# A hybrid attention and gated-linear-attention layer on one core: warm-up at the start, earlier tables, another layout of memory for the output passes, and projections ahead of the last products

## The chip, the cores and the metric

The kernel runs on one core of a Trainium2 chip. The metric is the device time of one execution in microseconds, and smaller is better. The core has a matrix engine (TensorE, PE in the profile), a vector engine (VectorE, DVE), an engine for activations (ScalarE, ACT), a general one (GpSimd, POOL) and a queue engine that issues the DMAs (SyncE, SP).

## The reference

2048 tokens of 1024 numbers go through one layer. `norm_mix`, `ple_norm` and `final_norm` are weights of root-mean-square norms.

```python
u = rmsnorm(h, norm_mix);  z = u @ w_in           # one projection for both groups
aq, ak, av, gq, gk, gv, g_low, za, zg = split(z)
aq, ak = partial_rope(aq, positions), partial_rope(ak, positions)   # sine and cosine tables
y_att = swa_sink_attention(aq, ak, av, sinks)     # window of 128 tokens
log_g = log_sigmoid(g_low @ w_gate_up + b_gate) / 16
y_gla = rmsnorm(gla_chunked(gq, gk, gv, log_g), gla_norm)
h = h + concat(y_att * silu(za), y_gla * silu(zg)) @ w_out
gate = sigmoid(rmsnorm(h, ple_norm) @ w_ple_gate)
out = rmsnorm(h + gate * (p @ w_ple_proj), final_norm)
```

Everything is float32. Each product is made of three products of a high and a low part of the operands.

## The kernel before, in words

The work has two phases. The first makes everything up to the gated outputs of both groups; the second is the output projection, the gate and the last norm.

**First phase.** The 16 tiles of 128 tokens are done in two halves of eight. For a tile, `u_norm` and `u_scale` (L328 to L342) norm the 128x1024 tile `xt`, and `u_tr` (L343) transposes it on TensorE and splits it into `uth` and `utl`. `load_w` (about L262 to L293) loads weights in pieces called `raw`, and splits each into a high part `wh` (ScalarE, L286) and a low part `wl` (VectorE or GpSimd, L288); the parts are also stored to `wd` in DRAM, for the second half. The first weights are `wA`, 272 columns wide: 256 for keys and values of the attention and 16 for `g_low`. `section_a` multiplies a tile by `wA`, turns the keys by the rotary tables `csC` and `csS`, splits them into `kst`, and transposes `kst` (L392). `constants()`, called inside the first `section_a`, loads small constants and `w_gate_up` (into `wu`, split to `wup`, L193 to L201) and makes the rotary tables (L204 to L244).

**Second phase.** Three passes: 0 and 1 add the two halves of the output projection to the residual, 2 makes the gate. A pass multiplies blocks of two row tiles (a pair; the first and, in passes 0 and 1, the last block have two pairs, n = 0 and 1) by a 1024x1024 weight with seven products in place of eight, in the order `ORDER = 0, 4, 1, 6, 5, 2, 3`. A product is 12 matmuls of 128x512 (L774 to L776). Its right operand `T` was made in the first phase and stored in DRAM; a T is loaded in four pieces of 512 KB (L122). Its left operand `c` comes from sums of pieces `y` (passes 0, 1) or `hT` (pass 2) on VectorE, split by ScalarE and VectorE. `xt` (L814) is the residual in passes 0 and 1, `u` (L829) holds product 0 for later. Pass 2 is `gate_block`: `load_p` loads a piece `pi` of the input `p` and transposes it (L901), `load_r` loads the residual `hr`, `proj` multiplies `pi` by `w_ple_proj` (L911 to L913, loaded and split by `load_wq`), `gated` makes sigmoid, product, sum and sum of squares, and `finish` scales by the last norm and stores. The last block does product 3 in two halves of 256 columns (`halves`).

**What sets the order.** The order on each engine is that of a scheduler which simulates the engines' times when the program is built and takes what it finds ready; the code's order sets what comes first among equals. On the chip each engine then works in this fixed order. SP issues nearly all DMAs, in order, on eight lanes in turn: a DMA waits for the one eight before it. Memory is handed out by pools; a tile in a pool waits until the tile that held its place is no longer used. Pools on the right side of the memory (`kvp`, `rawp`) are closed in the second half's last group, and that room goes to the second phase first.

## Time and profile before

| | us |
|---|---|
| median of 3 runs | 1906.24 (1900.41 to 1909.64) |
| profiled execution | 1904.04 |
| its span, first to last instruction | 1902.3 |
| TensorE busy | 1814.7 (95%) |
| VectorE, ScalarE, GpSimd busy | 1203.3, 961.1, 699.3 |
| mean granted clock of TensorE | 0.990 |

TensorE is busy nearly all the time, so what counts is where it is not and what released it then. In a row of the timeline the start comes first and then the duration of one instruction, or of a run of equal ones; `x8` is their number, and a bracket tells the idle time before it and which engine, tile and line ended it. Matmuls overlap, so a duration is longer than the distance to the next one. In a window's row the busy time of each engine stands with its number of instructions, and then the granted clock of TensorE (1.00 is full), the busy share of the DMA engines and GB/s. Rows of SP with `SPq` tell when a DMA was issued, not when it landed.

### The profile page before, as it was taken

The numbers are of one execution on the slowest core, as the hardware profiler recorded it, in microseconds if no ns is written. First come the engines' busy times: TensorE is split into PE (matmuls) and PEld (weight loads), VectorE is DVE, ScalarE is ACT, GpSimd is POOL, SyncE is SP. The second block draws the span as 40 slices with busy tenths as digits, with TensorE's granted clock in tenths as the row PEclk, the third lists the DMA queues.
The fourth block names the chain that finished last, engine by engine and source line by source line (L and its number), as shares of the span: only waits on it lengthen the run. The fifth ranks groups of instructions, "written<-read, shape, count | busy, mean of one in ns | idle before, by whom it ended". The sixth has DMA issues, their size and how long they took to land. (4 is left out here: it accounts for less than half of the span.)

```text
span 1902.3 us, 32715 instructions
## 1 busy us (share of the span) xinstructions
PE 1814.7 (95%) x11297; PEld 1612.9 (85%) x11297; DVE 1203.3 (63%) x2663; ACT 961.1 (51%) x2598; POOL 699.3 (37%) x916
## 2 busy tenths in 40 slices
PE   6999999999999999999999999999899999998997
PEld 6989898998898889898888988988788888787886
DVE  6454785466556474578766756574667667665864
ACT  5544666465557464456654655563422244453543
POOL 5442554534526362544455445352200010102432
PEclk9999999999999999999999999999999999999998
DMA  8332442415324352655576566565685966884542
GB/s 281 122 101 81 147 136 92 155 53 170 97 66 143 102 180 90 199 146 174 178 205 206 163 195 182 160 195 192 230 281 194 324 237 219 313 309 151 179 139 83
DMA packets 326741, 326.78 MB, mean 172 GB/s; under 512 B 23137, under 2 KB 259825, under 8 KB 326321
## 3 DMA queue, kind: packets, MB, share of 16 engines
q1 hardware_dynamic: 326576, 324.70, 52.5%
q8 instruction: 89, 1.46, 0.3%
q14 instruction: 76, 0.61, 0.1%
HBM read 186.08 MB, written 138.54 MB: 171 GB/s over the span
## 5 line engine op out<-in xcount | busy, mean ns | idle before, releaser
L85 PE MATMUL acc<-wh,uth 128*128 128x256 f32 (+1 forms) x1664 | 476.8, 287 | 14.5 <-DVE m L563 4.5
L86 PE MATMUL acc<-wl,uth 128*128 128x256 f32 (+1 forms) x1664 | 472.6, 284 | 6.2 <-DMA wl<-wd 6.0
L87 PE MATMUL acc<-wh,utl 128*128 128x256 f32 (+1 forms) x1664 | 471.1, 283 | 0.0
L85 PEld LDWEIGHTS acc<-wh,uth 128*128 128x128 f32 x1664 | 316.0, 190 | 25.6 <-ACT v L522 5.9
L86 PEld LDWEIGHTS acc<-wl,uth 128*128 128x128 f32 x1664 | 315.7, 190 | 12.9 <-DMA wl<-wd 8.6
L87 PEld LDWEIGHTS acc<-wh,utl 128*128 128x128 f32 x1664 | 315.7, 190 | 2.0
L460 POOL TENSOR_TENSOR pq<-pq,pmask 128x512 fp32r<-128x512 f32 x128 | 178.2, 1408 | 292.9 <-ACT pq L67 285.8
L85 PE MATMUL acc<-uth,wh 128*128 128x512 f32 x512 | 204.3, 399 | 4.8 <-DVE m L563 3.8
L87 PE MATMUL acc<-uth,wl 128*128 128x512 f32 x512 | 201.7, 394 | 0.3 <-DMA wl<-wd 0.3
L86 PE MATMUL acc<-utl,wh 128*128 128x512 f32 x512 | 201.9, 394 | 0.0
L774 PE MATMUL acc<-T,c 128*128 128x512 f32 (+1 forms) x344 | 135.5, 395 | 6.7 <-ACT u L829 6.3
L775 PE MATMUL acc<-T,c 128*128 128x512 f32 (+1 forms) x344 | 135.1, 393 | 0.0
L776 PE MATMUL acc<-T,c 128*128 128x512 f32 (+1 forms) x344 | 135.0, 393 | 0.0
L446 ACT ACTIVATE s<-s,sm 128x128 f32<-128x128 f32 x256 | 99.7, 391 | 51.1 <-DVE sm L442 51.1
L85 PEld LDWEIGHTS acc<-uth,wh 128*128 128x128 f32 x512 | 96.4, 188 | 26.8 <-DVE m L563 5.2
L859 POOL TENSOR_TENSOR ssh<-ssh 128x1 f32<-128x1 f32 x16 | 3.3, 205 | 313.8 <-ACT junk L858 313.8
L288 POOL TENSOR_TENSOR wl<-raw,wh 128x512 fp32r<-128x512 f32 (+1 forms) x82 | 109.6, 1367 | 20.0 <-ACT wh L286 10.2
L87 PEld LDWEIGHTS acc<-uth,wl 128*128 128x128 f32 x512 | 96.1, 188 | 22.5 <-DMA wl<-wd 0.7
L86 PEld LDWEIGHTS acc<-utl,wh 128*128 128x128 f32 x512 | 96.2, 188 | 18.7
L67 ACT ACTIVATE c<-s 128x512 fp32r<-128x512 f32 x72 | 45.1, 629 | 111.1 <-DVE s L104 32.4
L774 PE MATMUL o<-T,c 128*128 128x512 f32 (+1 forms) x252 | 99.3, 394 | 0.0
L775 PE MATMUL o<-T,c 128*128 128x512 f32 (+1 forms) x252 | 98.6, 391 | 0.0
(289 smaller groups left out, 4409.7 us busy)
## 6 DMA issues: line engine op xcount, KB each, us to landing
T<-td SPq DMA_DIRECT2D x84, 512.0 KB, 9.4
wd<-wh SPq DMA_DIRECT2D x20, 1024.0 KB, 5.6
wd<-wl SPq DMA_DIRECT2D x20, 1024.0 KB, 6.3
wh<-wd SPq DMA_DIRECT2D x80, 256.0 KB, 5.4
wl<-wd SPq DMA_DIRECT2D x80, 256.0 KB, 5.5
raw<-in_w_in SPq DMA_DIRECT2D x68, 256.0 KB, 5.6
y<-yts SPq DMA_DIRECT2D x64, 256.0 KB, 5.6
td<-th SPq DMA_DIRECT2D x48, 256.0 KB, 2.8
```

The lines of the kernel that those rows point to most:

```text
L67: act.activation(h, src, AF.Copy)
L85: pe.matmul(ps, lhs_h(k), rhs_h(k), start=(k == 0), stop=False)
L86: pe.matmul(ps, lhs_h(k), rhs_l(k), start=False, stop=False)
L87: pe.matmul(ps, lhs_l(k), rhs_h(k), start=False, stop=(k == nk - 1))
L288: eng.tensor_tensor(wl[:, ks_, 0:n], raw[:, :, 0:n], wh[:, ks_, 0:n], op=ALU.subtract)
L446: act.activation(s[:, j, :], s[:, j, :], AF.Exp, bias=ng[:, j:j + 1], accum_out=su[:, j:j + 1])
L460: pool.tensor_tensor(pq[:, 2 + i, :].rearrange("p (h n) -> p h n", h=4), pq[:, i, :].rearrange("p (h n) -> p h n", h=4), pmb, op=ALU.mult)
L774: pe.matmul(ps, c[:, 0, k, :], t[:, 0, k, sl], start=(first and k == 0), stop=False, skip_group_check=more)
L775: pe.matmul(ps, c[:, 0, k, :], t[:, 1, k, sl], start=False, stop=False, skip_group_check=more)
L776: pe.matmul(ps, c[:, 1, k, :], t[:, 0, k, sl], start=False, stop=(k == 3), skip_group_check=more)
L859: pool.tensor_tensor(ss[:, 0:1], ss[:, 0:1], ss[:, 1:2], op=ALU.add)
```

## The change

Six edits, all in how and when things are done; what is computed stays.

1. Ahead of everything, 14 matmuls of a zero tile `cold` (bfloat16, 128x512) run on TensorE.
2. The rotary tables become a function of their own, called right after the first tile's transposes and ahead of the norm of the third.
3. `load_w` loads new weights wider than 256 columns (only `wA`) in pieces of one 128-row block instead of two: 16 DMAs instead of 8. `raw` becomes a tile of 512 columns, with ten of them instead of nine.
4. The pools of the second phase: `tpr`, on the right, has room for two T instead of three, `tpb` for five instead of four; the tiles of `x2` (15 instead of 17) go to a pool on the right, opened with `tpr`; `c` and the tiles of `load_wq` have pools of their own; `pi` has a single buffer; the results `q` of `gate_block` go from `x2` to `x2b`.
5. `load_wq` moves from the last block of pass 1 to the block before it. The first `load_p` of a block moves to its start.
6. In the last block both projections come at product 6, ahead of products 5, 2 and 3; `finish` of the block's first row comes at product 2.

```diff
@@ start
+        cold = cp.tile([P, 512], BF16, name="cold")
+        dve.memset(cold, 0.0)
+        ps = pt("o")
+        for i in range(14):
+            pe.matmul(ps, cold[:, 0:P], cold, start=True, stop=True)
@@ pools' tiles
     def x2(name, shape=(P, 4, P), dtype=F32):
-        return p2p["xpb"].tile(list(shape), dtype, name=name, tag="x2", bufs=17)
+        return p2p["xpa"].tile(list(shape), dtype, name=name, tag="x2", bufs=15)
...
         for i in which:
-            T[i] = p2p["tpr" if i in ORDER[:3] else "tpb"].tile(
-                [P, 2, 4, 512], F32R, name=f"T{i}", tag="T", bufs=3 if i in ORDER[:3] else 4)
+            T[i] = p2p["tpr" if i in ORDER[:2] else "tpb"].tile(
+                [P, 2, 4, 512], F32R, name=f"T{i}", tag="T", bufs=2 if i in ORDER[:2] else 5)
...
-        rawp = kvs.enter_context(tc.tile_pool(name="rawp", bufs=9, side="right"))
+        rawp = kvs.enter_context(tc.tile_pool(name="rawp", bufs=10, side="right"))
@@ constants()
+        def rotary_tables():
 
             pos_f = wk.tile([16, P], F32, name="pos_f", tag="w1", bufs=8)
@@ load_w
-            for k0 in range(0, KD, 2):
-                ks_ = slice(k0, k0 + 2)
+            kn = 2 if n <= 256 or saved is not None else 1
+            for k0 in range(0, KD, kn):
+                ks_ = slice(k0, k0 + kn)
...
-                raw = rawp.tile([P, 2, SW], F32, name="raw", tag="raw")
+                raw = rawp.tile([P, 512], F32, name="raw", tag="raw")[:, 0:kn * n].rearrange("p (k n) -> p k n", k=kn)
...
-                eng = dve if fast and k0 % 4 == 0 else pool
+                eng = dve if fast and k0 % (2 * kn) == 0 else pool
@@ first phase
         u_tr(0, 0)
+        rotary_tables()
         u_norm(0, 2)
...
                     kvs.close()
-                    p2p["tpr"] = p2r.enter_context(tc.tile_pool(name="tpr", bufs=1, side="right", reuse_waits="tile"))
+                    for name in ("tpr", "xpa"):
+                        p2p[name] = p2r.enter_context(
+                            tc.tile_pool(name=name, bufs=1, side="right", reuse_waits="tile"))
                     T = [None] * 7
-                    load_T(0, ORDER[:3], T)
+                    load_T(0, ORDER[:2], T)
@@ second phase
-        for name in ("xpb", "tpb", "fs"):
+        for name in ("tpb", "cpl", "xpb", "wqp", "fs"):
             p2p[name] = p2.enter_context(tc.tile_pool(name=name, bufs=1, reuse_waits="tile"))
-        load_T(0, ORDER[3:], T)
+        load_T(0, ORDER[2:], T)
...
-            pi = x2("pi", (P, DPLE))
+            pi = fs.tile([P, DPLE], F32, name="pi", tag="pi", bufs=1)
...
-            qs = [[x2(f"q{i}", (P, 512)) for i in range(4)] for _ in prs]
+            qs = [[x2b(f"q{i}") for i in range(4)] for _ in prs]
...
                 elif i == 2:
-                    pps = proj(pTs[n, 0], banks())
+                    pps = state.get(0) or proj(pTs[n, 0], banks())
                     gated(n, 0, 0, pps, s2)
                     gated(n, 0, 1, pps, s2)
+                    finish(n, 0, s2)
                     if last:
-                        state["s"] = s2
-                        state["p"] = proj(pTs[n, 1], [pt("t"), pt("t")])
-                        state["s1"] = sums()
-                        gated(n, 1, 1, state["p"], state["s1"])
-                    else:
-                        finish(n, 0, s2)
+                        state["s"] = sums()
+                        gated(n, 1, 1, state[1], state["s"])
...
-                    if not posts and two:
-                        load_wq()
-                if i == (5 if two else 6):
-                    for h in range(1 if two else 2):
-                        pTs[n, h] = load_p(2 * prs[n] + h)
-                        hrs[n, h] = load_r(2 * prs[n] + h)
+                if i == 5 and two:
+                    hrs[n, 0] = load_r(2 * prs[n])
...
+            if two:
+                for n in range(2):
+                    pTs[n, 0] = load_p(2 * prs[n])
+            else:
+                for h in range(2):
+                    pTs[0, h] = load_p(2 * prs[0] + h)
+                    hrs[0, h] = load_r(2 * prs[0] + h)
             state = {}
...
-                gated(n, 1, 0, state["p"], state["s1"], slice(0, 256))
-                gated(n, 1, 0, state["p"], state["s1"], slice(256, 512), 2)
-                finish(n, 0, state["s"])
-                finish(n, 1, state["s1"])
+                gated(n, 1, 0, state[1], state["s"], slice(0, 256))
+                gated(n, 1, 0, state[1], state["s"], slice(256, 512), 2)
+                finish(n, 1, state["s"])
...
                 if i == 6:
                     state["b6"] = ps
+                    state[0] = proj(pTs[n, 0])
+                    state[1] = proj(pTs[n, 1], [pt("t"), pt("t")])
@@ loop over blocks
+            if ps_ == 1 and prs == (3,):
+                load_wq()
```

The scheduler turns these edits into another order. On SP at the start, before (`raw` are weights, `wd` the stores of split weights, `wu` the four loads of `w_gate_up`):

```order
L292 DMA wd_211<-wl 128x2176
L284 DMA raw<-in_w_in 128x2x128 x5
L292 DMA wd_280<-wh 128x8x256
L284 DMA raw<-in_w_in 128x2x128
L193 DMA wu_368<-in_w_gate_up 16x512 x4
L284 DMA raw<-in_w_in 128x2x128 x2
L292 DMA wd_280<-wl 128x8x256
L284 DMA raw<-in_w_in 128x2x256 x5
```

and now:

```order
L333 DMA xt<-in_x 128x1024
L293 DMA raw<-in_w_in 128x2x128 x8
L293 DMA raw<-in_w_in 128x2x256 x5
L301 DMA wd_355<-wh 128x8x256
L199 DMA wu_443<-in_w_gate_up 16x512 x2
L301 DMA wd_355<-wl 128x8x256
L199 DMA wu_443<-in_w_gate_up 16x512 x2
```

The loads of `wu` went behind seven more loads of weights (two of 128 KB and the five of 256 KB in the last row of before) and, two of them, behind the second store.

On SP around the start of the second phase, before (`xt` is the residual, `y` the left operand, `T` the right one; four pieces are one T):

```order
L814 DMA xt_17658<-in_x 128x512
L587 DMA yts_72<-oyg 128x256
L814 DMA xt_17660<-in_x 128x512
L814 DMA xt_17662<-in_x 128x512
L805 DMA y<-yts_61 128x512 x2
L805 DMA y<-yts_62 128x512 x2
L814 DMA xt_17698<-in_x 128x512
L814 DMA xt_17700<-in_x 128x512
L122 DMA T_17560<-td_145 128x2x512 x4
L122 DMA T_17565<-td_145 128x2x512 x4
L122 DMA T_17570<-td_145 128x2x512 x4
L122 DMA T_17575<-td_145 128x2x512 x4
```

and now:

```order
L128 DMA T_17606<-td_162 128x2x512 x3
L128 DMA T_17611<-td_162 128x2x512 x4
L128 DMA T_17616<-td_162 128x2x512 x4
L128 DMA T_17621<-td_162 128x2x512
L596 DMA yts_70<-oyg 128x256
L596 DMA yts_71<-oyg 128x256
L128 DMA T_17621<-td_162 128x2x512 x3
L817 DMA y<-yts_63 128x512 x2
L817 DMA y<-yts_64 128x512 x2
L596 DMA yts_72<-oyg 128x256
L826 DMA xt_17694<-in_x 128x512
L826 DMA xt_17696<-in_x 128x512
```

The first `xt` stood ahead of sixteen pieces of T and now stands behind twenty of them and behind four pieces of `y` of the third block; the twelve `y` of the first two blocks (yts_57 to yts_62) now stand ahead of all of these rows, behind the first two T.

On TensorE at the end of the program, before (`pp` and `t` are banks of the projections, `o` is one half of the last product 3):

```order
L911 MATMUL pp<-wph,pT 128x512
L912 MATMUL pp<-wpl,pT 128x512
L775 MATMUL o<-T_20048,c_21826 128x256
L776 MATMUL o<-T_20048,c_21826 128x256
L913 MATMUL pp<-wph,pT 128x512
L911 MATMUL pp<-wph,pT 128x512
L912 MATMUL pp<-wpl,pT 128x512
L913 MATMUL pp<-wph,pT 128x512
L911 MATMUL pp<-wph,pT 128x512
L912 MATMUL pp<-wpl,pT 128x512
L913 MATMUL pp<-wph,pT 128x512
```

and now, at the place where the projections end and product 5 begins:

```order
L924 MATMUL t<-wpl_19478,pT 128x512
L925 MATMUL t<-wph_19477,pT 128x512
L923 MATMUL t<-wph_19489,pT 128x512
L924 MATMUL t<-wpl_19490,pT 128x512
L925 MATMUL t<-wph_19489,pT 128x512
L786 MATMUL o<-T_20112,c_21865 128x512
L787 MATMUL o<-T_20112,c_21865 128x512
L788 MATMUL o<-T_20112,c_21865 128x512
```

The projections ended the program; now product 5 (T_20112), product 2 and both halves of product 3 come behind them, and the last matmul is one of product 3.

## Rows read from the trace of the kernel before

**Rows 1.** The page: busy time, share and instructions by engine; then TensorE in forty slices.
```profile
PE 1814.7 (95%) x11297; PEld 1612.9 (85%) x11297; DVE 1203.3 (63%) x2663; ACT 961.1 (51%) x2598; POOL 699.3 (37%) x916
...
PE   6999999999999999999999999999899999998997
```

**Rows 2.** Waits of TensorE, whole span: line, releaser, us in total, times, longest.
```profile
PE acc L774 <- ACT u L829: 6.3, 2, 4.5
...
PE t L392 <- DVE kst L373: 5.3, 1, 5.3
PE t L901 <- DMA pi<-in_p: 4.1, 1, 4.1
```

**Rows 3.** Timeline of TensorE, 10 to 20 us: start, duration, instruction.
```profile
15.21 0.43 PE L85 MATMUL acc<-wh,uth 128*128 128x272 f32 x1
...
19.08 0.29 PE L85 MATMUL acc<-wh,uth 128*128 128x272 f32 x1
```

**Rows 4.** DMA view, 0 to 40 us: issues, size each, median us to landing.
```profile
raw<-in_w_in SPq DMA_DIRECT2D x13, 256.0 KB, 5.4
...
raw<-in_w_in SPq DMA_DIRECT2D x4, 16.0 KB, 4.5
```

**Rows 5.** Timeline of ScalarE, 6 to 46 us, idle time before in brackets.
```profile
13.12 0.66 ACT L286 ACTIVATE wh<-raw 128x544 fp32r<-128x544 f32 x1 [0.93 <-DMA raw<-in_w_in]
...
40.83 1.28 ACT L238 ACT_TABLE_LOAD   x1
```

**Rows 6.** Timeline of VectorE, 34 to 46 us.
```profile
35.16 0.68 DVE L201 TENSOR_TENSOR wup<-wu,wu 16x512 fp32r<-16x512 f32 x1 [2.01 <-ACT wu L200]
...
44.37 0.29 DVE L373 TENSOR_TENSOR kst<-ks,kst 128x128 fp32r<-128x128 f32 x1
```

**Rows 7.** Window 50 to 55 us: busy by engine, granted clock, DMA share, GB/s.
```profile
50.00:55.00 5.00, 5.00 (x34) 5.00 (x34) 2.14 (x3) 1.75 (x3) 0.74 (x2) 0.73 0.14 54
```

**Rows 8.** Timeline of the DMA queue SP, 0 to 40 us.
```profile
26.50 3.34 SPq L193 DMA_DIRECT2D wu<-in_w_gate_up  x4
```

**Rows 9.** Timeline of TensorE, 1360 to 1380 us.
```profile
1367.68 0.80 PE L774 MATMUL acc<-T,c 128*128 128x512 f32 x1 [4.50 <-ACT u L829]
...
1378.77 0.39 PE L774 MATMUL acc<-T,c 128*128 128x512 f32 x1
```

**Rows 10.** Windows of 5 us behind that stretch.
```profile
1370.00:1375.00 5.00, 5.00 (x16) 4.01 (x15) 1.38 (x2) 0.63 (x1) 0.00 (x0) 0.63 1.05 391
...
1380.00:1385.00 5.00, 5.00 (x24) 4.14 (x23) 0.97 (x2) 0.54 (x1) 0.00 (x0) 1.00 1.05 387
```

**Rows 11.** Timeline of the DMA queue SP, 1300 to 1420 us.
```profile
1351.27 2.02 SPq L814 DMA_DIRECT2D xt<-in_x  x3
...
1363.01 17.91 SPq L122 DMA_DIRECT2D T<-td  x16
```

**Rows 12.** DMA view, 1345 to 1382 us.
```profile
T<-td SPq DMA_DIRECT2D x16, 512.0 KB, 10.8
...
xt<-in_x SPq DMA_DIRECT2D x10, 256.0 KB, 6.0
```

**Rows 13.** Timeline of the DMA queue SP, 1700 to 1735 us.
```profile
1722.43 0.88 SPq L1032 DMA_DIRECT2D raw<-in_w_ple_proj  x2
1723.37 0.42 SPq L897 DMA_DIRECT2D pi<-in_p  x1
```

**Rows 14.** Window 1730 to 1735 us.
```profile
1730.00:1735.00 5.00, 5.00 (x21) 4.01 (x20) 1.26 (x3) 1.19 (x3) 0.20 (x1) 0.79 0.53 186
```

**Rows 15.** Tile `pi`, 1715 to 1735 us: its loads from issue to landing.
```profile
DMA to landing us min/median/max: 4.2/4.5/5.0
```

**Rows 16.** Timeline of TensorE, end of the span.
```profile
1890.13 0.39 PE L913 MATMUL t<-wph,pT 128*128 128x512 f32 x1
```

**Rows 17.** Timeline of ScalarE, end of the span.
```profile
1893.65 1.33 ACT L940 ACTIVATE q<-q,rms 128x512 f32<-128x512 f32 x2
```

More of the change, by code (lines that the diff above doesn't have):

```diff
@@ L285, in load_w @@
                     o += m
-                act.activation(wh[:, ks_, 0:n], raw[:, :, 0:n], AF.Copy)
-                eng = dve if fast and k0 % 4 == 0 else pool
-                eng.tensor_tensor(wl[:, ks_, 0:n], raw[:, :, 0:n], wh[:, ks_, 0:n], op=ALU.subtract)
+                act.activation(wh[:, ks_, 0:n], raw, AF.Copy)
+                eng = dve if fast and k0 % (2 * kn) == 0 else pool
+                eng.tensor_tensor(wl[:, ks_, 0:n], raw, wh[:, ks_, 0:n], op=ALU.subtract)
             if saved is None:
@@ L600, in piece @@
             def piece(name, dtype=F32):
-                return rawp.tile([P, 2 * SW], dtype, name=name, tag="raw")[:, 0:512].rearrange("p (b n) -> p b n", b=4)
+                return rawp.tile([P, 4, P], dtype, name=name, tag="raw")
             def load(ps_, k, c):
@@ L765, in combos @@
                     src = {0: a11, 4: s_, 1: a12, 6: a21, 5: s_, 2: s_, 3: a22}[i]
-                    C[i] = p2p["xpb"].tile([P, 2, 4, P], F32R, name=f"c{i}", tag="c", bufs=8)
+                    C[i] = p2p["cpl"].tile([P, 2, 4, P], F32R, name=f"c{i}", tag="c", bufs=8)
                     split(C[i][:, 0], C[i][:, 1], src)
@@ L1021, in hybrid_block_kernel, with wqt @@
         wq_, fn = [], []
+        def wqt(name, dtype=F32):
+            return p2p["wqp"].tile([P, 512], dtype, name=name, tag=name)
         def load_wq():
             for n, ns in enumerate(NS):
-                fn.append(x2b(f"fn{n}"))
+                fn.append(wqt(f"fn{n}"))
                 nc.sync.dma_start(fn[n], final_norm[ns].partition_broadcast(P))
@@ L1029, in load_wq @@
                 for ns in NS:
-                    hl = [x2b(f"wp{c}", dtype=F32R) for c in "hl"]
+                    hl = [wqt(f"wp{c}{k}{len(wq_[k])}", F32R) for c in "hl"]
                     raw = x2("raw3", (P, 512))
```

## The prediction

> **What bounds the kernel now.** The page first: TensorE is busy for 1814.7 of 1902.3 us, and its row of forty slices is below 9 only at the start, in slice 31 and at the end [rows 1]. A change that leaves the matmuls alone can win at most the 87.6 us in which TensorE is idle, and what the clock loses behind a long idle stretch. The waits of TensorE say which idle time this change can touch [rows 2]: 5.3 us for `kst`, 4.5 of the 6.3 us for `u`, and 4.1 us for `pi`. The middle, where the order of instructions is the same before and now, I cost at no change. Timeline and windows then price each place.
>
> **Start, warm-up.** The first 128x272 matmuls take 0.43 us, later ones 0.29 us [rows 3]: TensorE at the lower and at the higher of its two clock levels. Where this is seen again with 512 columns (below), the matmuls follow each other 0.427 against 0.2265 us apart, 0.2 us more each; for 272 columns that is 0.107. I count 23 of them and 16 transposes that run slowly: 2.5 us, and with the transposes at most 4.2. The fourteen zero matmuls run while nothing else can; at 0.427 us each they are done after some 6 us, ahead of the first tile. But the clock is not all. The first weights come in sixteen DMAs instead of eight, and a DMA of SP waits for the one eight before it. 16 KB loads of `raw` land in 4.5 us where the 256 KB ones need 5.4 [rows 4], so halving a load hardly shortens its turn: eight more turns of 4.5 us on eight lanes are 4.5 us if all of it shows, and nothing if the shorter transfers and the overlap make it good. The last piece of these weights is split at 13.12 us now [rows 5]; I expect 15 to 16. TensorE would then wait where it now runs slowly. I take a gain of 2 us, bounds a loss of 2 and a gain of 4.2.
> "DMA: Bandwidth & Descriptors" in the Trainium skill (Rules for kernel authors) says that many small transfers should be made one large one, since below 64 KB one pays mostly overhead; the 4.5 us of the 16 KB load agree with it. By that rule alone the split costs the whole 4.5 us, and the start loses 0.3 us instead of gaining 2; by the bytes alone it would gain 4.2.
>
> **Start, rotary tables.** TensorE waits 5.3 us for `kst`, which VectorE writes at 44.37 [rows 2, 6]. Just ahead VectorE stood 2.0 us for `wu` [rows 6], and the tables go through a table load of 1.28 us on ScalarE at 40.83 [rows 5]. Behind the wait the clock is at the lower level for a while, a mean of 0.73 still in 50 to 55 us [rows 7]. Some 36 matmuls there cost 0.1 us more each, 3.6 us, and TensorE idles 0.8 us again. That is 9.7 us for the whole place. Now the tables are made between the first tiles' transposes, some 20 us earlier on VectorE, so that stall goes. What is late next is `wu`: its four loads were issued at 26.50, in 3.34 us [rows 8]; now seven more loads of weights, 1.5 MB, stand ahead of them on SP, for two of them a store of 1 MB too, and ScalarE takes `wu` ahead of `kst`. Eight DMAs more at the 0.84 us that an issue takes in that row, and the eight of the split, make some 7 to 10 us, so about 35 us, while TensorE, with 24 us of work from 11 us on, asks for `kst` at 35 to 38. A stall of 0 to 3 us may stay. I take 6 us gained, bounds 1 and 9.7. Both parts of the start together: 8 us.
>
> **From the first to the second phase.** TensorE idles 4.5 us until 1367.68 [rows 2, 9]: `u` (ScalarE) stands behind copies that wait for VectorE. Behind it the window 1370 to 1375 holds 16 matmuls at a granted clock of 0.63, 1380 to 1385 holds 24 at 1.00 [rows 10]; 13 slow ones at 0.2 us more are 2.6 us. So 7.1 us can go. After the change `y` of the first two blocks (twelve loads of 256 KB) goes out some 45 us earlier, so VectorE has less to do here, and I expect this stall to go. But what was ahead is now behind. Of the seven T only two instead of three are loaded ahead, and SP issues twenty pieces of T of 512 KB (10.5 MB) before the first residual `xt`; before, ten `xt` loads were issued from 1351.27 on, ahead of the sixteen pieces at 1363.01 [rows 11]. The DMA engines carry 387 GB/s here at a share of 1.05, so they are full [rows 10]. From about 1347, when room is free for T, 10.5 MB of T, 1.05 MB of `y` and 0.25 MB of `xt` need 11.8 / 0.387 = 30.5 us: the first `xt` is there at about 1378. TensorE has 84 matmuls, 19 us, that need no `xt`, from 1350.5 to 1369.5; product 5 then waits for a bank that VectorE frees only with `xt`. So a new idle stretch of 10 us, until about 1380, and 2.6 us of lower clock behind it. Before, product 5 began at 1378.77 [rows 9]: a loss of 4 us. Bounds: a gain of 7 if `xt` comes in time, as it would if each load took the 6.0 us that `xt` took here before [rows 12], and a loss of 8 if T starts later. Once this is over all T are there, and nothing is late behind it.
> In the Trainium skill, "DMA: Bandwidth & Descriptors" (Queues, rings and completion order) says that on each DMA engine the descriptors of one queue are taken in ring order. By that an `xt` gets no share ahead of T, and the 4 us are lost; without it the 7 would be gained. The 10.8 us of T beside 6.0 us of `xt` [rows 12] do not decide, since no `xt` stood behind so much T.
>
> **Second to third pass.** TensorE idles 4.1 us for `pi` [rows 2], which SP issues at 1723.37, behind the loads of `w_ple_proj` [rows 13]. Behind the wait the clock is 0.79 in 1730 to 1735 [rows 14]; 8 matmuls at 0.2 us more are 1.6 us. Now `w_ple_proj` comes a pass earlier, and so does the first `pi`. With some of the smaller waits there I take 6 us gained, bounds 3 and 9. What hides the rest: `pi` has one buffer now, and SP waits in order until it is free. From one transpose of `pi` to the next TensorE has 26 matmuls or more, 5.9 us; a load of `pi` landed in 4.2 to 5.0 us [rows 15]. So I cost the single buffer at nothing, with 0.9 us of room at the tightest place.
>
> **Tail.** TensorE's last matmul starts at 1890.13, and the span ends 11.8 us after it is over; in between ScalarE scales two pieces of `q` in 1.33 us from 1893.65 on, for the first row of the last block [rows 16, 17]. Now the 24 projection matmuls (5.4 us) stand ahead of product 5, and that row is finished ahead of the last halves. There are as many matmuls; behind the last one there remain an addition, sigmoid, product, sum, sum of squares, scale and store: 9.3 to 9.8 us by the pieces of before. 2 us gained, bounds 0 and 3.
>
> **Sum.** -8 + 4 - 6 - 2 = -12 us. The profiled execution took 1904.04 us (its span 1902.3 and 1.7 around it), 2.2 less than the median of 1906.24. So 1892 from the one and 1894 from the other: **1893 us**.
>
> **Rivals.** (a) The sum as above: 45%. (b) Nothing that can be told: the split loads eat the warm-up and `wu` holds `kst` (-3 for the start instead of -8), and the transition loses 8: -3 + 8 - 6 - 2 = -3, so 1902. For it: DMA is full at both places. Against it: `pi` and the tail hang on neither. 27%. (c) More: `xt` comes in time, -8 - 7 - 6 - 2 = -23, so 1882. For it: `xt` landed in 6.0 us before under the same load; against it the order of SP. 18%. (d) Slower: the single buffer of `pi`. If a load of it lands more than 5.9 us after the transposes before it, SP stands, with `hT` of the next block and `hr` behind it, and TensorE idles in each of six blocks as it now does once, 4.1 us and 1.6 of lower clock: 34 us, 1927. If half the blocks are hit, 1910. Against it: a DMA share of 0.53 there [rows 14], and loads within 5.0 us so far. 10%, of which 7 are slower than the bound.
>
> About 0.5%, 9.5 us, is what a measurement of this kernel can tell from no change: faster is below 1896.7, slower above 1915.8. Of (a) 43 parts of 45 are faster, and (c) with all its 18, and 3 of (b): 64%. Slower 7%, the same 29%. The range goes from (c) to the middle of (b) and (d): 1881 to 1905; that of (a) alone is 1887 to 1899.
>
> **What would show it.** Right: 272-column matmuls of 0.29 us soon after the first, no wait for `kst` over 3 us, granted clock 1.00 in 45 to 55 us; a wait of 8 to 11 us near 1369 that an addition of `xt` on VectorE ends; no wait for `pi`; less than 10.5 us from the last matmul to the end. Wrong: no idle stretch near 1369 (then c); a wait for the first weights, or for `kst` as long as now (then b); a wait for `pi` or `hT` in each block of the third pass (then d).

## The result: slower by half a per cent, not faster

| us | median (runs) | profiled execution, its span |
|---|---|---|
| before | 1907.55 (6) | 1904.04, 1902.3 |
| changed | 1918.50 (6) | 1920.28, 1918.6 |

The ratio is 1.0064 [1.0040, 1.0087], and 1.0055 [1.0037, 1.0072] in a second measurement. 1893 was forecast, in a range up to 1905: the time is outside it, on the side that had a chance of 7%.

To see where it goes I compare the two traces at equal work: for a moment of the kernel before I add up the columns that its matmuls have streamed, and look when the changed kernel has streamed as many (its zero matmuls not counted). The difference is TensorE's lag in us (negative: it is ahead).

| at (us, kernel before) | 24 | 47 | 55 | 100 | 1350 | 1390 | 1722 | 1755 | 1890 |
|---|---|---|---|---|---|---|---|---|---|
| changed | 4.0 | 3.0 | 2.2 | 6.3 | 14.9 | 21.3 | 24.1 | 16.0 | 16.2 |
| before, another execution (e5) | -0.3 | 0.3 | 1.1 | 1.1 | 1.6 | 2.4 | 3.8 | 3.4 | 3.4 |

So the start costs 6.3 us, the long middle 8.6, the transition 6.4, the second pass 2.8; `pi` gives back 8.1; from 1755 to the end nothing changes. These make 16.0 of the 16.3 us by which the spans differ. Of the start's 6.3 us, 2.2 are there at 55 us; the other 4.1 come between 65 and 84 us.

### The profile page after: what moved, and what is told of

It is laid out like the page before. It is cut to its first block, busy times and chain, and to the rows that moved or that the text cites. A ratio compares the mean times of both kernels' runs of the same rounds, so it can differ in the third digit from the quotient of the medians.

```text
span 1918.6 us, 32723 instructions
## 1 busy us (share of the span) xinstructions
PE 1827.5 (95%) x11311; PEld 1619.8 (84%) x11311; DVE 1215.2 (63%) x2666; ACT 963.4 (50%) x2602; POOL 700.5 (37%) x918
## 4 chain that ended last, share of the span: by engine, by line
PE 36%; DMA 7%; DVE 5%; ACT 3%; issue 1%; SPq 1%; POOL 0%; DVEq 0%; ACTq 0%; POOLq 0%
PE acc L91 4%; PE acc L92 4%; PE acc L93 4%; PE acc L786 3%; PE acc L788 3%; PE acc L787 3%; PE o L788 2%; PE o L786 2%; PE o L787 2%; DMA y<-yts 1%; DMA wh<-wd 1%; DMA T<-td 1%; PE sw L788 1%; PE sw L786 1%; PE sw L787 1%
```

## The profile after

The page's first row and TensorE's slices, against [rows 1]:

```profile
PE 1827.5 (95%) x11311; PEld 1619.8 (84%) x11311; DVE 1215.2 (63%) x2666; ACT 963.4 (50%) x2602; POOL 700.5 (37%) x918
...
PE   7999999999999989999989999999889999999997
```

TensorE is busy 12.8 us longer, of which the zero matmuls are 6. Its waits (in total, times, longest), against [rows 2]:

```profile
PE acc L786 <- DVE xt L113: 11.4, 2, 10.8
...
PE t L401 <- DVE kst L382: 3.4, 1, 3.4
...
PE t L355 <- DVE utl L74: 2.3, 2, 1.2
PE t L355 <- DVE xt L348: 1.8, 2, 1.4
```

The wait for `pi` is gone, and so is the long one for `u`. `kst` is still waited for, `xt` of the second phase is now waited for 10.8 us, and the first tiles (`utl`, `xt` L348) have waits of their own.

**Start.** Timeline of TensorE, against [rows 3]:

```profile
5.47 1.75 PE L67 MATMUL o<-cold 128*128 128x512 bf16 x4
7.62 1.32 PE L355 MATMUL t<-identr,xt 128*128 128x128 f32 x8 [0.40 <-DVE xt L348]
10.53 0.59 PE L91 MATMUL acc<-wh,uth 128*128 128x272 f32 x1 [1.59 <-ACT uth L73]
...
12.77 0.28 PE L215 MATMUL t<-identr,pos_f 16*128 16x16 f32 x1 [1.42 <-DVE utl L74]
...
13.38 0.43 PE L91 MATMUL acc<-wh,uth 128*128 128x272 f32 x1
...
17.18 0.29 PE L92 MATMUL acc<-wl,uth 128*128 128x272 f32 x1
...
21.94 0.63 PE L355 MATMUL t<-identr,xt 128*128 128x128 f32 x4 [1.36 <-DVE xt L348]
23.72 0.90 PE L355 MATMUL t<-identr,xt 128*128 128x128 f32 x4 [1.16 <-DVE utl L74]
...
24.65 0.43 PE L91 MATMUL acc<-wh,uth 128*128 128x272 f32 x1
```

The warm-up works: the eight transposes end after 1.32 us. Before, they took 1.97:

```profile
7.46 1.97 PE L346 MATMUL t<-identr,xt 128*128 128x128 f32 x8 [7.46 <-DVE xt L339]
```

Then TensorE has nothing to do, since `uth` and `utl` of the first tile are not there, and the 272-column matmuls begin at the pace of the lower level all the same. Two waits later, from 24.65 on, they are slow once more. The windows (busy by engine PE, PEld, DVE, ACT, POOL; granted clock; DMA share; GB/s) say so too:

```profile
10.00:15.00 5.00, 3.05 (x12) 2.69 (x13) 4.59 (x10) 3.25 (x8) 3.51 (x5) 0.53 0.69 172
...
20.00:25.00 5.00, 2.49 (x16) 2.07 (x15) 4.97 (x9) 1.63 (x6) 3.93 (x6) 0.90 1.03 397
25.00:30.00 5.00, 5.00 (x34) 5.00 (x33) 3.58 (x15) 4.16 (x12) 3.71 (x11) 0.76 0.90 275
...
50.00:55.00 5.00, 4.75 (x23) 4.35 (x23) 4.25 (x6) 3.32 (x9) 2.98 (x10) 0.53 0.34 105
```

VectorE is busy for 4.97 of the 5 us from 20 to 25 while TensorE has half a window's work: the early tables stand among the first tiles. The last row is behind the wait for `kst`; it answers to [rows 7]. What was late there is on the queue SP, against [rows 8]:

```profile
4.59 7.95 SPq L293 DMA_DIRECT2D raw<-in_w_in  x13
12.59 0.43 SPq L333 DMA_DIRECT2D xt<-in_x  x1
...
34.38 1.48 SPq L199 DMA_DIRECT2D wu<-in_w_gate_up  x2
...
37.16 3.32 SPq L199 DMA_DIRECT2D wu<-in_w_gate_up  x2
```

And on ScalarE:

```profile
43.47 0.28 ACT L372 ACTIVATE ks<-acc 128x128 f32<-128x128 f32 x1 [5.55 <-PE acc L93]
...
43.92 0.61 ACT L204 ACTIVATE wup<-wu 16x512 fp32r<-16x512 f32 x1
```

`xt` at 12.59 is the third tile, behind thirteen pieces of weights; `wu` is issued between 34.4 and 40.5, and ScalarE splits it at 43.92, ahead of `kst`.

**Transition.** The queue SP, against [rows 11]:

```profile
1364.66 12.99 SPq L128 DMA_DIRECT2D T<-td  x12
...
1385.05 3.49 SPq L817 DMA_DIRECT2D y<-yts  x4
...
1389.65 7.39 SPq L826 DMA_DIRECT2D xt<-in_x  x10
```

TensorE, against [rows 9]:

```profile
1386.01 0.39 PE L788 MATMUL sw<-T,c 128*128 128x512 f32 x1
1397.23 0.79 PE L786 MATMUL acc<-T,c 128*128 128x512 f32 x1 [10.83 <-DVE xt L113]
1397.82 0.63 PE L787 MATMUL acc<-T,c 128*128 128x512 f32 x1
```

The first `xt` is issued only behind all of T and four `y`, and product 5 begins at 1397.23, which is 1382.3 without the lag of 14.9 that was there already. Behind it the matmuls follow each other 0.427 us apart: the lower level.

**Pass 2 and the tail.** The window that answers to [rows 14] is at full clock without an idle stretch:

```profile
1730.00:1735.00 5.00, 5.00 (x28) 4.13 (x27) 2.72 (x5) 1.51 (x4) 0.00 (x0) 1.00 0.28 105
```

At the end, one row each of TensorE, ScalarE, GpSimd and VectorE; the last matmul starts 12.2 us before the span's end, as in [rows 16] (1902.3 less 1890.13):

```profile
1906.34 0.28 PE L788 MATMUL o<-T,c 128*128 128x256 f32 x1
...
1910.23 1.32 ACT L952 ACTIVATE q<-q,rms 128x512 f32<-128x512 f32 x2
...
1911.40 2.93 POOL L953 TENSOR_TENSOR q<-q,fn 128x512 f32<-128x512 f32 x2
...
1911.46 3.41 DVE L955 SCALAR_TENSOR_TENSOR q<-q,rms,fn 128x512 f32<-128x512 f32 x2 [0.95 <-POOL rms L79]
```

ScalarE's two scalings of the block's first row come at the very end here as in [rows 17], and now GpSimd's and VectorE's last work falls together.

## The experiments

Each median stands beside that of the kernel before, run on the same chip in between. Lags are TensorE's, as above.

### The start: e1, e2, e3, e12

e1 is the changed kernel without edits 1 to 3 (`rotary_tables()` is back in `constants()`):

```diff
-        for i in range(14):
-            pe.matmul(ps, cold[:, 0:P], cold, start=True, stop=True)
...
-            kn = 2 if n <= 256 or saved is not None else 1
+            kn = 2
...
-        rotary_tables()
```

> The changed kernel with the first three edits undone (no zero matmuls, rotary tables back inside the constants, first weights in eight DMAs); the memory of the second phase, pi and the tail stay changed. Theory A (the start loses because the sixteen DMAs push the third tile's load and the loads of wu back): TensorE's lag behind the kernel before, which is 6.3 us at 100 us in the changed kernel, is within 0.5 us of zero there, and the time falls by 6 us to about 1912. If the extra lag of the middle (6.3 to 12 us between 100 and 1300 us) only follows from the start, it goes too: 1907. Rival B (the start is slow for another reason, for example the pool of raw tiles or the other layout): the lag at 100 us stays at 4 us or more, 1917 to 1919.

Measured: 1912.14 (10) against 1910.13 (26), ratio 1.0003 [0.9986, 1.0020]. The lag at 100 us is 0.4 and not 6.3, the 5.3 us for `kst` are back, and the 10.6 us for `xt` stay. The three edits of the start lose time; the rest is about even.

e2 keeps the zero matmuls and the early tables, and takes back the split alone (`kn = 2`).

> The changed kernel with one edit undone: the first weights in eight DMAs again (raw tiles of 544 columns, nine of them). Theory A: the third tile's load is issued at about 10 us instead of 12.6, the waits of 1.4 and 1.2 us at 21 to 24 us go, the loads of wu are issued at about 27 us instead of 34 to 40, and the wait for kst falls under 1 us; the lag at 100 us falls from 6.3 us to between -4 and 0, the time to 1908 to 1912. Rival C (the early rotary tables take VectorE's time just when it is needed for the tiles): the waits at 21 to 24 us stay, lag at 100 us of 4 us or more, 1916 or more.

Measured: 1913.77 (10), ratio 1.0018 [1.0008, 1.0028]. Timeline of SP in e2:

```profile
4.95 4.76 SPq L293 DMA_DIRECT2D raw<-in_w_in  x5
9.75 0.47 SPq L333 DMA_DIRECT2D xt<-in_x  x1
...
27.43 2.25 SPq L199 DMA_DIRECT2D wu<-in_w_gate_up  x4
```

And of TensorE:

```profile
24.61 1.11 PE L355 MATMUL t<-identr,xt 128*128 128x128 f32 x4 [4.11 <-DVE utl L74]
```

With eight DMAs the third tile is issued at 9.75 and `wu` at 27.43, and no wait for `kst` is left: the split made both late. But now the tables stand in VectorE's way, 4.11 us for `utl`. The lag is 7.1 at 24 us, -2.0 at 55 and 0.9 at 100: early tables and zero matmuls together gain no more than they cost (e1 has 0.4 at 100 us). Taking back the split alone removes 5.4 of the start's 6.3 us. "DMA: Bandwidth & Descriptors" in the Trainium skill (Rules for kernel authors) has it that many small transfers should be one large one; this trace agrees, with 2.8 us more until SP comes to the third tile.

One thing more makes the tables dear here. Two of their rows on VectorE in e2, of one form:

```profile
16.89 0.28 DVE L238 SCALAR_TENSOR_TENSOR ra_t<-ra_t 128x128 f32<-128x128 f32 x1
...
21.46 1.34 DVE L239 SCALAR_TENSOR_TENSOR ra_t<-ra_t 128x128 f32<-128x128 f32 x1
```

And what GpSimd does beside the second:

```profile
19.18 4.74 POOL L297 TENSOR_TENSOR wl<-raw,wh 128x512 fp32r<-128x512 f32 x3
```

The row beside GpSimd's splits takes 1.06 us more, and it stands ahead of the `utl` that TensorE waits for. No run takes GpSimd's work away here; e16 below does so at the end of the program.

e3 keeps all of the changed kernel and loads and splits `wu` ahead of the first weights.

```diff
+        def gate_up():
...
+        gate_up()
```

> The changed kernel with one edit more: the four loads of w_gate_up and their split go ahead of the first weights' loads. Theory A: the wait for kst at 47 us (3.4 us) goes, and with it the lower clock in 47 to 54 us (about 4 us); the waits at 21 to 24 us stay or grow by 1 to 2 us, since four more DMAs stand ahead of the third tile. Lag at 100 us 1 to 3 us instead of 6.3, time 1912 to 1915. Rival (kst is late for its own tile, not for wu): the wait for kst stays at 3 us or more, 1918.

Measured: 1915.43 (10), ratio 1.0025 [1.0013, 1.0038]. No wait for `kst`; in its place one of 5.2 us for `uth` at 14.02, since ScalarE splits `wu` first (its timeline):

```profile
12.72 0.62 ACT L209 ACTIVATE wu<-wu 16x512 fp32r<-16x512 f32 x1
13.37 0.60 ACT L73 ACTIVATE uth<-t 128x512 fp32r<-128x512 f32 x1
```

The lag is 4.6 at 24 us, -2.9 at 55 and -0.2 at 100: with the split and the early tables still there, the start's loss is gone once `wu` stands ahead. The third tile is issued at 14.35 here, later than in the changed kernel; so what the split costs is the place of `wu`. (This trace then loses 12.6 us in the middle, from 100 to 1350.)

e12 leaves out the zero matmuls alone.

> The changed kernel without the fourteen zero matmuls (the sixteen DMAs and the early tables stay). Theory A (they gain next to nothing: the clock they bring up is lost again in the waits at 9 to 13 us): lag at 20 us within 0.7 us of the changed kernel's, time the same, 1916 to 1920. Rival (they gain the 2 us forecast for the start): 2 us slower or more, 1920 to 1922.

Measured: 1916.06 (12) against 1909.86 (35), ratio 1.0032 [1.0018, 1.0046]; the changed kernel's intervals overlap with this. The lag is 0.4 at 19 us and 4.1 at 20, where the changed kernel has -0.5 at both: the warm clock gives 0.9 us until 19. The other 3.7 at 20 are a wait that e12 has begun by then and the changed kernel meets a little later, in two parts (1.36 and 1.16 above):

```profile
23.18 0.66 PE L352 MATMUL t<-identr,xt 128*128 128x128 f32 x4 [3.28 <-DVE utl L71]
```

At 24 us e12 has 5.4 against 4.0, at 47 us 1.4 against 3.0, at 100 us 3.2 against 6.3: the gain is gone, and more. In e12 no wait for `kst` is left, though `wu` is issued as late as in the changed kernel (35.4 to 40.5); without the zero matmuls the engines' orders differ, and no run separates the two.

### The transition: e4, e6

e4 opens the pool of the residual first, so that it gets the room that comes free first:

```diff
-        for name in ("tpb", "cpl", "xpb", "wqp", "fs"):
+        for name in ("xpb", "tpb", "cpl", "wqp", "fs"):
```

> The changed kernel with the order of the second phase's pools changed alone: the pool of the residual pieces xt is opened ahead of that of T, so that it gets the room that is free first. SP then issues seven xt ahead of twenty T pieces. Theory A (xt is late since its room, and so its loads, come behind 10.5 MB of T): the wait of 10.8 us for the addition of xt goes, TensorE waits at most 2 us for T instead, the transition's lag falls by 9 to 12 us, time 1907 to 1910. Rival D (the DMA engines are full here, so whatever is put ahead the last comes as late): TensorE waits 5 us or more for T in place of xt, time 1914 to 1918.

Measured: 1917.20 (5), ratio 1.0039 [1.0024, 1.0053]. Timeline of SP in e4:

```profile
1355.77 3.76 SPq L826 DMA_DIRECT2D xt<-in_x  x5
...
1367.93 16.72 SPq L128 DMA_DIRECT2D T<-td  x15
```

And of TensorE:

```profile
1403.47 0.47 PE L786 MATMUL sw<-T,c 128*128 128x512 f32 x1 [1.95 <-issue]
```

`xt` is issued ahead of T now, and the wait of 10.8 us is gone. Part of it comes back: 2.1 us for a `y`, 1.0 for a `c`, and the 2.0 of this row, for which the profile names no releaser. It is not T, whose last piece landed at 1395.58. Just ahead of it VectorE reads the bank `sw`, and before that it stood for a `y`:

```profile
1402.08 0.69 DVE L113 TENSOR_TENSOR s<-y 128x512 f32<-128x512 f32 x1 [1.49 <-DMA y<-yts]
1402.68 0.68 DVE L113 TENSOR_TENSOR xt<-xt,sw 128x512 f32<-128x512 f32 x1
```

It is one of the four `y` of a block that SP issues from 1393.76 on, and from 1385.05 on in the changed kernel. From 1350 to 1420 the lag grows by 3.1 us and not by 6.4 (and by 3.5 in e6 below, where e1 has 4.9). So the order in which room comes free put `xt` behind T, and up to half of the cost goes with it; some of the rest is that `y` comes later now. The time does not show it: the interval overlaps with the changed kernel's, and 1907 to 1910 did not come.

e6 is e1 and e4 together, the changed kernel without its two losses.

> The start of the kernel before (no zero matmuls, rotary tables in the constants, eight DMAs) together with the residual pool ahead of that of T; early y, early pi, early w_ple_proj and the changed tail stay. Theory A: no lag at 100 us, transition 1 to 5 us better than the run with the old start alone, 5 us better from pi: 1902 to 1906, a ratio to before of 0.996 to 0.998. Rival (each gain comes back as a wait for T): ratio 1.000 or more.

Measured: 1908.71 (12) against 1907.64 (29), ratio 1.0003 [0.9990, 1.0016]: even with the kernel before, the rival's ratio. In its trace the transition still costs 3.5 us and the second pass 4.3, which is nearly the 8.1 that `pi` gives back.

### The tail: e7, e16

e7 is e6 with the old order of the last block.

```diff
-                    state[0] = proj(pTs[n, 0])
-                    state[1] = proj(pTs[n, 1], [pt("t"), pt("t")])
...
+                        state["p"] = proj(pTs[n, 1], [pt("t"), pt("t")])
```

> As the run with old start and residual room, with the last block's projections and the finish of its first row where the kernel before has them. Theory A (the changed tail gains nothing: the chain behind the last matmul is as long as before, since product 5, 2 and 3 now end closely behind each other and VectorE and ScalarE have the work of three products behind the last matmul): the same time within 1 us, 11.8 us from the last matmul to the end in both. Rival (it gains the 2 us forecast): 2 us slower.

Measured: 1907.09 (12), ratio 1.0001 [0.9983, 1.0020]: the new tail gains nothing. The last scalings of VectorE in e7:

```profile
1900.05 1.41 DVE L952 SCALAR_TENSOR_TENSOR q<-q,rms,fn 128x512 f32<-128x512 f32 x2 [0.94 <-POOL rms L76]
```

0.7 us each, where the changed kernel takes 1.7. In e16, e6 again, GpSimd's two multiplications by the last norm's weight are left out, so that one row tile lacks that factor.

```diff
                         act.activation(o, o, AF.Copy, scale=rs2)
-                        pool.tensor_tensor(o, o, fn[j], op=ALU.mult)
```

> The changed kernel with the old start and the residual's room first (e6), and in the last block GpSimd's two multiplications by the last norm's weight left out, so that row lacks that factor. In e6 VectorE's last two scalings take 3.41 us (1.7 each), beside two of GpSimd (2.93 us) at the same time; with the old tail, where GpSimd is done before, 1.41 us. Theory A, the new tail's missing 2 us are the two engines in each other's way: VectorE's pair takes 1.4 to 1.5 us, and from the start of the last matmul to the end of the span it is 10.6 to 11.0 us instead of 12.8. Rival, the pair is slow because of something else that stands there (ScalarE's scalings just ahead, the stores): it stays at 3.4, and the end at 12.4 to 12.8 us.

Measured in one execution: span 1899.5. Its last matmul:

```profile
1889.19 0.28 PE L785 MATMUL o<-T,c 128*128 128x256 f32 x1
```

And VectorE's last scalings:

```profile
1894.32 1.41 DVE L952 SCALAR_TENSOR_TENSOR q<-q,rms,fn 128x512 f32<-128x512 f32 x2 [0.95 <-POOL rms L76]
```

1.41 us again, and 10.3 us from the last matmul to the end, where e6 has 12.8 and e7 10.6. The two engines stood in each other's way; without that the new order would be about even with the old one on this kernel, and 1.9 us better than [rows 16] have it (12.2). The old order too ends 10.0 to 10.6 us behind its last matmul in every trace with `pi` in its own buffer (e7, e9, e10, e11, e13, e14); what shortens it there no run isolates. "SBUF — State Buffer" in the Trainium skill (SBUF: two separate sides) says that VectorE and GpSimd share a pair of ports which one holds for a whole instruction while the other is blocked; e16 agrees with it, with 2.0 us for the pair.

### `pi` and the late `wu`, on the kernel before: e9, e13, e8, e10, e11, e14

e9 is the kernel before with `pi` early and in a buffer of its own.

```diff
-            pi = x2("pi", (P, DPLE))
+            pi = fs.tile([P, DPLE], F32, name="pi", tag="pi", bufs=1)
...
+            if two:
+                for n in range(2):
+                    pTs[n, 0] = load_p(2 * prs[n])
```

> The kernel before with one part of the fifth edit alone: pi has its own buffer and a block's first load of it stands at the block's start (w_ple_proj stays where it was, in the last block of pass 1). Theory A (pi was the whole stall between pass 1 and 2, and one buffer costs nothing): the wait of 4.1 us for pi and the lower clock behind it go, 5 to 7 us less lag from 1722 to 1755 us, time 1900 to 1903, ratio 0.996 to 0.9975. Rival (the early pi only shows the next wait, for w_ple_proj's split or hT): less than 2 us.

Measured: 1913.03 (12) against 1909.86 (35), ratio 1.0009 [0.9996, 1.0023]. The wait for `pi` is gone, and the next one takes its place (waits of TensorE):

```profile
PE t L911 <- ACT wph L67: 4.3, 1, 4.3
```

The lag grows by 7.0 us from 1722 to 1755. e13 adds the early `w_ple_proj`, with the room that it needs (15 tiles of `x2`, `q` in `x2b`).

```diff
+            if ps_ == 1 and prs == (3,):
+                load_wq()
```

> The kernel before with pi early in its own buffer and w_ple_proj loaded and split in pass 1, in a pool of its own (room from two fewer x2 tiles; q in x2b); T, y and xt as before, start and tail as before. Theory A (pi and w_ple_proj were one chain: each alone only shows the other): no wait over 1 us for pi or wph at 1720 to 1735 us, 6 to 9 us less lag from 1700 to 1755 us, no loss at the transition: ratio 0.995 to 0.997. Rival (the early loads and fewer x2 tiles take as much elsewhere, as in the changed kernel between 1590 and 1700 us, 3 us there): ratio 0.998 or more.

Measured: 1901.37 (12) against 1905.29 (25), ratio 0.9968 [0.9952, 0.9983]. Neither wait is left, and from 1722 to 1755 the lag falls by 8.0 us. `pi` alone does not bring it, both loads together do; `w_ple_proj` alone was not run. They have a price ahead of that: from 1420 to 1722 the lag grows by 1.9 to 5.0 us in all thirteen traces with both loads early (2.8 in e13), and by 0.2 to 1.4 in the four without.

e8, e10 and e11 move the four DMAs of `wu` alone: in e8 (on e6) and e10 (on e9) right behind the first weights, in e11 (on e9) behind the loads of the third and fourth tile.

```diff
+        wus = [w2("wu0")]
+        for i in range(4):
+            nc.sync.dma_start(wus[0][32 * i:32 * i + 16, :], w_gate_up)
```

> As the run with old start and residual room, and the four loads of w_gate_up issued right behind the first weights, ahead of the third tile, nothing else moved. Theory A (in the kernel before it was VectorE's wait for wu and the late table load behind it that held kst): the wait for kst of 5.3 us falls to 0 to 2.5 us and the lower clock behind it goes or shortens: 3 to 8 us faster than that run. Against it: the third tile comes 3 us later and may make TensorE wait 1 to 2 us at 20 us. Rival (the tables themselves are late, whatever wu does): wait for kst stays above 4 us, no gain.

> The kernel before with pi early and with the loads of w_gate_up right behind the first weights, ahead of the third tile (as in the run with wu behind the weights). Theory A (the two places are independent): 3 to 6 us less from the start beside the 5 to 7 us of pi: 1895 to 1899, ratio 0.992 to 0.996. Rival (the start's gain is given back in the middle, where that run had fallen back from -3.6 to +2.0 us by 1330 us): no better than pi alone.

> As the run before this one, but the loads of w_gate_up stand behind the third and fourth tiles' loads. Theory A (the wait of 2.3 us at 20 us in the run with wu behind the weights came from the third tile pushed back by 3 us): no wait over 1 us at 18 to 24 us, wu is still in time, and the lag at 100 us is 1 to 3 us lower than with wu ahead of the third tile. Rival (wu comes too late again there): a wait for kst of 2 us or more.

Measured: e8 1904.49 (12) against 1907.64 (29), 0.9982 [0.9969, 0.9994], where e6 had 1.0003; e10 1908.88 and e11 1908.11 (12 each) against 1909.86 (35), 0.9998 [0.9985, 1.0011] and 0.9993 [0.9979, 1.0007], where e9 had 1.0009. In all three the wait for `kst` is gone and the lag at 55 us is near -6; e8 has waits of 3.5 us and e10 of 3.0 us for `utl` instead, where ScalarE and VectorE split `wu` early; e11 has 1.2. With the tables where they were, the 5.3 us of [rows 2] hung on where `wu` stands in the queue. Early tables remove them too: e2 has no such wait either, with `wu` at 27.43, about where the kernel before has it. One of the two is enough.

e14 is e13 with `wu` as in e11.

> As the run before, and the loads of w_gate_up behind the third and fourth tiles' loads. Theory A: -4 us at 100 us beside the gain between the passes, ratio 0.992 to 0.996, faster than the kernel before beyond the interval, best of all so far. Rival (gains at the start are lost in the middle): no better than the run before.

Measured: 1898.35 (8) against 1905.29 (25), ratio 0.9957 [0.9941, 0.9972]. It beats both kernels; against e13 the intervals overlap. The 4.7 us by which it leads at 100 us are gone by 1350 (0.8 behind), and so are the 3.4 and 4.0 of e10 and e11 (0.8 and 2.8 behind). TensorE is 7.4 us ahead at 55 us, and the windows behind both places are at full clock:

```profile
50.00:55.00 5.00, 4.75 (x41) 4.51 (x40) 4.18 (x11) 2.90 (x9) 4.10 (x10) 1.00 0.00 0
...
1730.00:1735.00 5.00, 5.00 (x24) 4.14 (x23) 4.79 (x10) 1.28 (x4) 1.25 (x3) 1.00 0.89 311
```

### Both kernels once more: e5, e15

> The kernel before, unchanged, once more with a profile. The changed kernel's TensorE falls back by another 8.6 us between 100 and 1350 us, where the order of instructions is the same as before. Theory A (this part is no effect of the edits: short stretches at the lower clock and waits of 1 to 2 us that come or stay away from one execution to the next): against the first trace of the kernel before this one lags by 3 us or more somewhere in the middle, with other stretches of lower clock. Rival (the edits slow the middle): the two traces of before agree within 1 us at 1330 us.

> The changed kernel once more, on the same chip as the other runs of this group. Theory A: start +6 and transition +6, passes -5, tail 0, and the middle only varies: ratio 1.003 to 1.005 (6 to 9 us), with another trace's middle between 2 and 9 us. Rival (the middle's 8.6 us belong to the change): ratio 1.006 or more and a middle of 8 us again.

e5 took 1907.44, e15 1917.36 (12 runs) against 1905.29 (25). The second trace of the changed kernel has the same lags, 6.3 at 100 us and 14.8 at 1350; the second trace of before is 3.4 us behind the first, 0.5 of it from 100 to 1350, so theory A of e5 does not get its 3 us in the middle. Over all 123 runs the kernel before has a median of 1908.44: its first profiled execution, at 1904.04, was a quick one by 4.4 us, and the changed kernel's, at 1920.28, was 1.8 above its median; some 6 of the 16.3 us are that.

## Why the prediction was wrong, step by step

| term | forecast | trace |
|---|---|---|
| start | -8 | +6.3 |
| middle | 0 | +8.6 |
| transition | +4 | +6.4 |
| second pass | 0 | +2.8 |
| `pi` | -6 | -8.1 |
| tail | -2 | 0 |

- **Start: the step that failed.** It is 14.3 of the 28 us between the forecast's sum of -12 and the 16.0 of the trace. By 24 us, ahead of the place of `kst`, TensorE is 4.0 us behind where 2 ahead was forecast; over that place, until 55 us, it wins 1.8 us and not 6; and 4.1 more are lost by 84 us. Two costs were not in it.
  - The tables were "some 20 us earlier on VectorE", at no price. VectorE is full there, and e2 shows 4.11 us for it. All six traces with early tables lag by 3.6 to 7.1 us at 24 us, with the split or without it, with the zero matmuls or without; the others by 2.7 at most.
  - The split was priced by when the first weights are there. That came out (their last piece is split at 14.37, with 15 to 16 forecast), though not for the reason given: a halved load did land sooner, the 128 KB ones in 2.5 us and the 8 KB ones in 2.2, where the whole ones take 5.0 and 4.5. What the split delays is what stands behind it on SP, and there `wu`: I had it at about 35 us and a rest of 0 to 3 us; it came at 34.4 to 40.5 and left 3.4, with the clock at 0.53 behind it. e2 and e3, where `wu` comes early enough, are at 0.9 and -0.2 at 100 us.

  The warm clock was credited as if TensorE kept busy after the first transposes; it waits at 10.53 and 12.77, and the clock is low again. That early tables end the long wait for `kst` was right (e2), but so does an earlier `wu` alone (e8, e10, e11), at a lower price (lags of 2.7 us and less at 24 us). What takes the last 4.1 us is open: e2 and e3, without a wait for `kst`, lose 3.2 us there too. Rival (b) came nearest, with `wu` holding `kst` and the warm-up eaten, at too small a price and without the tables.
- **Transition: right in mechanism, a little short in size.** An idle stretch of 10 us until about 1380 was forecast, and 10.8 until 1382.3 (lag taken off) came, ended by `xt`. What I did not see is why: the room of the residual's pool, which the trace of e4 shows. Rival (c) is wrong for this kernel.
- **`pi`: right,** -8.1 for -6. The place needs `w_ple_proj` as well (e9 against e13). The second pass pays for it, 2.8 us, which the sum had at nothing: with both it is -5.3. Rival (d) did not come: no wait for `pi` in pass 2.
- **Tail: wrong.** The chain behind the last matmul was added up from durations of before, and in the new order two engines do their last work at once, and that takes back the 2 us (e16). Nor is the old order's end always as long as in the first trace: in e7 it is 10.6 us, in e9 10.0.
- **Middle: cost at nothing, since the order there is the same.** It is 8.6 and 8.5 us in the two traces of the changed kernel. How much of it is the change stays open. Kernels with the early tables lose 6.0 to 12.6 us there (six traces), those without -1.4 to 6.8 (eleven); but e6 and e16, alike up to the tail, differ by 4.6 us in it, at 3.2 and -1.4. The medians of e2 and e1, between which the early tables and the zero matmuls lie, differ by 1.6 us. Their traces are 8.8 us apart, for e2's execution was 2.7 us above its median and e1's 4.7 below. The other terms make 7.4 us, and the medians of the changed kernel are 11.0 and 12.1 us above those of before; that would leave some 4 us for the middle, an estimate from these numbers. No run isolates it.
- **The anchor.** I took 1906.24 and 1904.04 for the kernel before, and 1908.44 is its median over many runs.

## What to carry to other kernels

A load that is split, or put earlier, is paid by what stands behind it on its queue: read the queue's order up to the next transfer on which the bound engine's work hangs, even a small one (`wu`), and price its delay. Before moving work earlier, ask what the engine that does it is busy with at that time; the cheaper way to end a wait is often to move the one transfer that holds it (`wu`, four DMAs of 32 KB). And where two loads are late at one place, moving one can just show the other (`pi`, then `w_ple_proj`). A single trace can be some us off its kernel's median, so a small term is better read from several.

## What the runs showed of the hardware that was not expected

- Fourteen matmuls of zeros raise the clock (eight transposes take 1.32 us behind them and 1.97 without), and behind two waits of 1.6 and 1.4 us with little work between them it is low again: granted 0.53 from 10 to 15 us.
- At the very start the granted clock does not tell the pace. In e12, without zero matmuls, the window says 1.00, and its 272-column matmuls take 0.43 us until 17 us, as in the kernel before [rows 3]:

```profile
10.00:15.00 5.00, 2.00 (x7) 1.64 (x8) 4.55 (x8) 3.32 (x9) 3.32 (x4) 1.00 0.74 156
```

  One row of its timeline:

```profile
16.70 0.43 PE L89 MATMUL acc<-wl,uth 128*128 128x272 f32 x1
```

- Executions of one program differ in their mean granted clock, and the time goes with it: in the experiments the kernel before took 1913.2 us in the median of 9 runs at 0.986, and 1907.4 in 16 runs at 0.990.
- Two multiplications on GpSimd slow two scalings on VectorE from 0.7 to 1.7 us each (e16).
